# Preparing weight parts early and parking them in HBM: nine weight pairs of each FFN down projection in a float32 transformer trunk

## The chip, the cores and the metric

The kernel runs on one core of a Trainium2 chip. The metric is the device time of one execution in microseconds, taken as the median of repeated runs.

## The reference

Two post-norm layers over 256 positions of width 2048, all in float32. Each layer has a token mixer and a gated feed-forward network (FFN):

```python
for i in range(2):
    m = gmlp_mixer(x, ...) if i == 0 else mla_mixer(x, ...)
    x = layer_norm(ALPHA * x + m, ln_mix_g[i], ln_mix_b[i])
    f = conv_ffn(x, ...)
    x = layer_norm(ALPHA * x + f, ln_ffn_g[i], ln_ffn_b[i])

def conv_ffn(x, w_up, conv_w, conv_b, w_down):    # 2048 -> 2 x 5504 -> 2048
    h = causal_depthwise_conv3(x @ w_up, conv_w) + conv_b
    a, g = jnp.split(h, 2, axis=-1)
    return (jax.nn.silu(g) * a) @ w_down
```

The first mixer is a gMLP: `x @ w_in` (2048 to 12288), GELU, one half (v) normalized and mixed over 128-position windows, times the other half (u), then `w_out` (6144 to 2048). The second is multi-head latent attention.

## The kernel before

Float32 products are made from two parts. A value is split into a high part, rounded to the matmul's number format (a cast on ScalarE), and a low part, the rest (a subtraction on VectorE). A product is then three matmuls: high by high, low by high, high by low.

*Weights.* They are read once, in the order of use, as a list of chunks of 128 x 2048 (1 MB). The class `Feed` carries each through three steps: `_load` starts the transfer on SyncE's (SP's) queue into a tile `raw`; `_split` makes `wh` (L107, ScalarE) and `wl` (L108, VectorE); the caller uses the parts in matmuls (all recorded at L167). `feed.next(splits, loads)` keeps two to three chunks split and two more loaded ahead of the one in use. All these tiles, and the large activations too, come from one pool of 22 slots of 8 KB per partition (`big`), so a tile can start only when an older one in its slot is done with. The framework's scheduler settles the order of instructions on each engine and adds all semaphore waits.

*Down projections.* `down` makes a back projection (the gMLP's output, 48 blocks of k, or an FFN's second product, 43 blocks) in two halves of 1024 columns. A *unit* is a pair of k blocks in one half: a chunk of 2 x 1024 columns. Two blocks of k times two row blocks times two column blocks is a 2 x 2 matrix product, and there are two ways to make it. `Banks.eight` does the eight block products, 24 matmuls of 512 columns. `Banks.seven` uses seven products (a Strassen-Winograd form), 21 matmuls. It needs sums of weight blocks (`ts`, L122) and their parts `th`, `tl` besides `wh`, `wl` (L115, L116, in `Feed._seven`), and sums of activation blocks with their parts (`combine`). Eight PSUM banks take the products: four DIRECT ones (q3, p2, e, q4) and four OWN ones (p1, q5, p7, p6) that only the seven-product units use and that `rest` combines after the half's last one.

Which units use seven products is a table (`BACK`): 7 in each half of the gMLP's output, 6 in each half of an FFN's. The v part of the gMLP's first product uses them as well (`V_PAIRS`, `V_SEVEN`). The parts of the activations are made by the class `Sums`, four k blocks at a time (`quad`), and the sums for a pair once (`make`).

*Up projections.* 22 groups of output columns, four chunks each (the last two), with 256 positions as the moving operand: 16 matmuls of 512 and 16 of 256 columns per chunk. Convolution, SiLU and the product go into `act` tiles, six per FFN.

*Between them.* `boundary` finishes a normalization while the next product starts. `Norm` keeps the residual in two `big` slots; `restore` brings it back with the norm's scale and bias rows, during the next stage.

Of the kernel before, what the change touches and what calls it, by code (L numbers as in the profile page):

```python
# [15 lines left out]
P = 128  # L16
S = 256
# [42 lines left out]
def halves(n_k):  # L60

    one = [tuple(range(k, min(k + 2, n_k))) for k in range(0, n_k, 2)]
    two = []
    for q in BACK[n_k][1]:
        two += one[2 * q : 2 * q + 2][:: -1 if q in BACK[n_k][2] else 1]
    return [one, two]


class Feed:
# [3 lines left out]
    def __init__(self, nc, pool, chunks):  # L73
        self.nc, self.pool, self.chunks = nc, pool, chunks
        self.raw, self.parts = {}, {}
        self.loaded = self.split = self.used = 0

    def _load(self):
        ap, cols = self.chunks[self.loaded][:2]
        t = self.pool.tile([P, 2048], F32, tag="big", name=f"raw{self.loaded}")  # L80
# [12 lines left out]

    def _split(self):
        i = self.split
        cols, kind = self.chunks[i][1:]
# [5 lines left out]
        hi = self.pool.tile([P, 2048], F32R, tag="big", name=f"wh{i}")  # L102
        lo = self.pool.tile([P, 2048], F32R, tag="big", name=f"wl{i}")
# [14 lines left out]
    def _seven(self, i, raw):  # L118
# [4 lines left out]
        tile = lambda name, dt: self.pool.tile([P, 2048], dt, tag="big", name=f"{name}{i}")  # L123
# [8 lines left out]
        return wh, wl, th, tl  # L132

# [16 lines left out]
def trunk(ctx: ExitStack, tc: tile.TileContext, x, xT, gm_in, gm_wout, ffn_up, ffn_dn,  # L150
# [4 lines left out]
    big = ctx.enter_context(tc.tile_pool(name="big", bufs=22))  # L155
# [4 lines left out]
    def slot(shape, name, dt=F32):  # L160
        return big.tile(shape, dt, tag="big", name=name)
# [8 lines left out]
    chunks = []  # L170
# [6 lines left out]
    def back(w, n_k):  # L177

        for hf, units in enumerate(halves(n_k)):
            c = slice(hf * 1024, (hf + 1) * 1024)  # L180
            for u in units:
                if len(u) == 1:
                    chunks.append((w[u[0], :, c], 1024, "wide"))
                else:
                    chunks.append((w[u[0] : u[0] + 2, :, c].rearrange("k p c -> p k c"), 2048,
                                   "seven" if u[0] in BACK[n_k][0] else "wide"))

# [11 lines left out]
    feed = Feed(nc, big, chunks)  # L199

    idle = cpool.tile([P, 512], BF16, name="idle")
# [6 lines left out]

    def combine(name, o, k1, k2):


        t = tp.tile([P, 4, P], F32, tag="t2", name=f"xs{name}", bufs=6)
        b0, b1 = slice(0, P), slice(P, S)
        nc.vector.tensor_tensor(t[:, 0], k1[:, b1], k2[:, b1], ALU.subtract)
        nc.vector.tensor_tensor(t[:, 1], t[:, 0], k1[:, b0], ALU.subtract)
        nc.vector.tensor_tensor(t[:, 2], k1[:, b0], k1[:, b1], ALU.subtract)
        nc.vector.tensor_tensor(t[:, 3], k2[:, b0], t[:, 1], ALU.add)
# [3 lines left out]
        return [(o[:, 0, i], o[:, 1, i]) for i in range(4)]  # L221
# [40 lines left out]
    ones = cpool.tile([P, P], F32, name="ones")  # L262
    nc.gpsimd.memset(ones, 1.0)
# [45 lines left out]
    def sum_halves(acc, name):  # L309
        lo = tp.tile([P, S], F32, tag="t1", name=f"lo_{name}", bufs=8)  # L310
        nc.scalar.copy(lo, acc[:, S : 2 * S])  # L311
        h = tp.tile([P, S], F32, tag="t1", name=f"h_{name}", bufs=8)
# [3 lines left out]
    def split_act(src, name):  # L316

        t = tp.tile([P, 2 * S], F32R, tag="t2", name=name, bufs=6)
# [11 lines left out]
    class Banks:  # L330
# [17 lines left out]
        def seven(self, a, sums, wh, wl, th, tl):  # L348
            s1, s2, s3, s4 = sums
            self.to("p1", a[0][0], wh, wl, 0)  # L350
            self.to("q5", s1, th, tl, 0)
            self.to("p7", s3, th, tl, 512)
            self.to("p6", s2, th, tl, 1024)
            self.to("q3", s4, wh, wl, 512)
            self.to("p2", a[0][1], wh, wl, 1024)
            self.to("q4", a[1][1], th, tl, 1536)

        def rest(self):

            acc = self.acc  # L360
            p1, u2, u3, w, d = [tp.tile([P, 512], F32, tag="t2", name=f"{self.tag}{n}", bufs=6)
# [8 lines left out]
    class Sums:  # L370

        def __init__(self, src, tag):
            self.src, self.tag, self.rooms, self.got, self.quads = src, tag, [], {}, {}
            self.parts = {}

        def first(self):

            for k in range(4):  # L380
                x = self.src[0][:, k, :]
                t = tp.tile([P, 512], F32R, tag="t2", name=f"{self.tag}f{k}", bufs=6)
                nc.scalar.copy(t[:, 0:S], x)
                nc.vector.tensor_tensor(t[:, S : 2 * S], x, t[:, 0:S].bitcast(F32), ALU.subtract)
                self.parts[k] = t
            self.quads[0] = None

        def quad(self, q, n_k):
            if q in self.quads:
                return  # L390
            n = min(4, n_k - 4 * q)
            x = self.src[q // 2][:, 4 * (q % 2) : 4 * (q % 2) + n, :]
            t = slot([P, 4, 512], f"{self.tag}a{q}", F32R)
            nc.scalar.copy(t[:, 0:n, 0:S], x)
            nc.vector.tensor_tensor(t[:, 0:n, S : 2 * S], x, t[:, 0:n, 0:S].bitcast(F32), ALU.subtract)
            self.quads[q] = t
            for k in range(4 * q, 4 * q + n):
                self.parts[k] = t[:, k % 4, :]

        def make(self, k):  # L400
            if k in self.got:
                return
            n = len(self.got)
            if n % 2 == 0:
                self.rooms.append(slot([P, 2, 8 * P], f"{self.tag}xc{n}", F32R))
            x8 = self.src[k // 8]
            self.got[k] = combine(f"{self.tag}{n}", self.rooms[-1][:, n % 2, :], x8[:, k % 8, :], x8[:, k % 8 + 1, :])

    def down(n_k, src, tag, ln, sums, skew=SKEW):


        ln.begin()
        quads, sevens = sums.quads, BACK[n_k][0]
        late = []
        for hf, units in enumerate(halves(n_k)):
            n = len(units)
            last = [u for u in units if u[0] in sevens][-1]


            acc = Banks(f"{tag}{hf}", OWN + DIRECT if hf else DIRECT + OWN)  # L420
            for i, u in enumerate(units):
                left = n - 1 - i if hf == 1 else n
                for u2 in units[i : i + 3]:
                    sums.quad(u2[0] // 4, n_k)
                if i + 1 < n and units[i + 1][0] in sevens:
                    sums.make(units[i + 1][0])
# [3 lines left out]
                a = [[(sums.parts[k][:, b * P : (b + 1) * P], sums.parts[k][:, S + b * P : S + (b + 1) * P])  # L430
                      for k in u] for b in range(2)]
                if left < skew:
                    late.append((a, *got))
                elif u[0] in sevens:
                    acc.seven(a, sums.got[u[0]], *got)
# [3 lines left out]
                else:  # L439
                    acc.eight(a, *got)  # L440
                for q in [q for q in quads if q < u[0] // 4 and q not in [v[0] // 4 for v in units[i:]]]:
                    quads.pop(q)
            if hf == 0:
                for j, m in enumerate(DIRECT):
                    ln.piece(j // 2, j % 2, acc.acc[m])
                for q in [q for q in quads if q < units[-1][0] // 4]:
                    quads.pop(q)
# [68 lines left out]
    class Norm:  # L516


        def __init__(self, idx, res, last=False):
            self.idx, self.res, self.last, self.new = idx, res, last, None  # L520
            self.folded = set()

        def begin(self):
            if self.res is None:
                self.res = []
                for b in range(2):
                    t = slot([P, D], f"res{b}")
                    nc.sync.dma_start(t, x[b * P : (b + 1) * P, :])
                    self.res.append(t)
            self.stats = [st.tile([P, 4, 6], F32, tag="lnst", name=f"lnst{self.idx}_{b}") for b in range(2)]  # L530

# [11 lines left out]
        def restore(self, b, f):  # L543

            c = slice(f * 512, (f + 1) * 512)
            r = self.res[b][:, c]
            nc.vector.tensor_tensor(r, r, self.g[:, c], ALU.mult)
            nc.vector.tensor_tensor(r, r, self.b[:, c], ALU.add)

        def fold(self, b, f, part):  # L550

            r = self.res[b][:, f * 512 : (f + 1) * 512]
# [3 lines left out]
        def piece(self, b, f, acc):  # L556
            r = self.res[b][:, f * 512 : (f + 1) * 512]
# [12 lines left out]
        def scale(self, b, f):  # L570
            c = slice(f * 512, (f + 1) * 512)
            r = self.res[b][:, c]
# [587 lines left out]
```

## Time and profile before

| | |
|---|---|
| median of 3 runs | 2492.54 us (2492.25 to 2492.92) |
| the profiled execution | 2493.04 us, with a span of 2491.3 us |
| TensorE (PE) matmuls | 2475.7 us busy, 99% of the span |
| VectorE (DVE) | 1908.8 us, 77% |
| ScalarE (ACT) | 1388.8 us, 56% |
| GpSimd (POOL) | 2.9 us, no transfers issued |
| transfers | 480.27 MB, mean 193 GB/s |

The profile lists busy time for each engine, the chain of work that ended last, groups of instructions with their mean duration and the idle time before them, and transfers by issuing line with the time until the data has landed. The stretches by time from the span's start: v part of the gMLP to about 258 us, u part to 552, gMLP output to 800, first FFN up projection from 835 to 1285, its down projection to 1508, attention to 1770, second FFN up from 1804 to 2255, its down projection to the end.

### The profile page before, as it was taken

The numbers are of one execution on the slowest core, as the hardware profiler recorded it, in microseconds if no ns is written. First come the engines' busy times: TensorE is split into PE (matmuls) and PEld (weight loads), VectorE is DVE, ScalarE is ACT, GpSimd is POOL, SyncE is SP. The second block draws the span as 40 slices with busy tenths as digits, with TensorE's granted clock in tenths as the row PEclk, the third lists the DMA queues.
The fourth block names the chain that finished last, engine by engine and source line by source line (L and its number), as shares of the span: only waits on it lengthen the run. The fifth ranks groups of instructions, "written<-read, shape, count | busy, mean of one in ns | idle before, by whom it ended". The sixth has DMA issues, their size and how long they took to land.

```text
span 2491.3 us, 32651 instructions
## 1 busy us (share of the span) xinstructions
PE 2475.7 (99%) x13028; PEld 2128.3 (85%) x13028; DVE 1908.8 (77%) x2553; ACT 1388.8 (56%) x1891; POOL 2.9 (0%) x17
## 2 busy tenths in 40 slices
PE   9999999999999999999999999999999999999998
PEld 7888888888888888888888888988888888888886
DVE  7999866678888777666778997866487676669897
ACT  6566544445565755554655566565565555546553
POOL 0000000000000000000000000000000000000000
PEclk9999999999999999999999999999999999999999
DMA  7555554555566655555546674444465455555554
GB/s 295 198 187 214 196 186 157 181 196 194 186 217 222 223 186 200 188 184 185 187 155 201 219 247 169 168 153 168 156 231 191 169 202 182 180 179 179 209 192 181
DMA packets 86456, 480.27 MB, mean 193 GB/s; under 512 B 7712, under 2 KB 8480, under 8 KB 46752
## 3 DMA queue, kind: packets, MB, share of 16 engines
q1 hardware_dynamic: 86304, 478.19, 54.4%
q8 instruction: 102, 1.67, 0.3%
q14 instruction: 50, 0.41, 0.1%
HBM read 476.07 MB, written 2.10 MB: 192 GB/s over the span
## 4 chain that ended last, share of the span: by engine, by line
PE 96%; DVE 2%; issue 1%; DMA 1%; ACT 0%; SPq 0%; DVEq 0%; ACTq 0%
PE up L167 37%; PE u L167 11%; PE dn_q L167 9%; PE dn_p L167 6%; PE wo_q L167 4%; PE v_q L167 4%; PE mo L167 4%; PE dn_e L167 3%; PE v_p L167 3%; PE wo_p L167 3%; PE upf L167 2%; PE wo_e L167 2%; PE v_e L167 1%; PE mkv L167 1%; PE kn L167 1%; PE mq L167 1%
## 5 line engine op out<-in xcount | busy, mean ns | idle before, releaser
L108 DVE TENSOR_TENSOR wl<-raw,wh 128x1024 fp32r<-128x1024 f32 (+3 forms) x651 | 899.8, 1407 | 158.6 <-ACT wh L107 115.5
L107 ACT CAST wh<-raw 128x1024 fp32r<-128x1024 f32 (+3 forms) x651 | 761.8, 1201 | 284.9 <-DVE wl L108 120.4
L167 PE MATMUL up<-xhl,wh 128*128 128x512 f32 x2624 | 611.0, 390 | 0.0
L167 PEld LDWEIGHTS up<-xhl,wh 128*128 128x128 f32 x2624 | 487.4, 188 | 97.8
L167 PEld LDWEIGHTS up<-xhl,wl 128*128 128x128 f32 x2624 | 325.8, 192 | 6.4
L167 PE MATMUL up<-xhl,wl 128*128 128x256 f32 x2624 | 328.1, 283 | 0.0
L115 ACT CAST th<-ts 128x1536 fp32r<-128x1536 f32 x116 | 121.1, 1051 | 118.6 <-DVE ts L122 103.9
L167 PE MATMUL u<-xhl,wh 128*128 128x512 f32 x768 | 183.8, 393 | 0.3 <-DVE h_u L313 0.2
L167 PEld LDWEIGHTS u<-xhl,wh 128*128 128x128 f32 x768 | 141.3, 188 | 30.8 <-PE s L167 2.1
L116 DVE TENSOR_TENSOR tl<-ts,th 128x1536 fp32r<-128x1536 f32 x116 | 138.6, 1219 | 5.3 <-ACT th L115 4.5
L115 ACT CAST wh<-raw 128x1536 fp32r<-128x1536 f32 x58 | 85.9, 1480 | 43.2 <-DMA raw<-in_ffn_dn_dram 15.2
L116 DVE TENSOR_TENSOR wl<-raw,wh 128x1536 fp32r<-128x1536 f32 x58 | 101.6, 1752 | 5.4 <-ACT wh L115 5.4
L167 PEld LDWEIGHTS u<-xhl,wl 128*128 128x128 f32 x768 | 95.6, 192 | 2.0
L167 PE MATMUL u<-xhl,wl 128*128 128x256 f32 x768 | 96.7, 283 | 0.0
L167 PE MATMUL mo<-wh,oT 128*128 128x512 f32 x256 | 82.9, 404 | 0.0
L122 DVE TENSOR_TENSOR ts<-ts,raw 128x512 f32<-128x512 f32 x116 | 79.8, 688 | 1.8
L167 PE MATMUL wo_q<-wh,woa 128*128 128x512 f32 x256 | 78.8, 389 | 0.0
L122 DVE TENSOR_TENSOR ts<-raw 128x1024 f32<-128x1024 f32 x58 | 70.8, 1220 | 4.6 <-PE u L167 1.6
L313 DVE TENSOR_TENSOR h_0a<-up,lo_0a 128x256 f32<-128x256 f32 x41 | 17.3, 421 | 72.7 <-ACT lo_0a L311 72.7
L313 DVE TENSOR_TENSOR h_1a<-up,lo_1a 128x256 f32<-128x256 f32 x41 | 17.3, 421 | 71.9 <-ACT lo_1a L311 71.9
L167 PE MATMUL dn_q<-wh,dn0a 128*128 128x512 f32 x232 | 71.7, 390 | 0.0
L167 PE MATMUL dn_q<-wh,dn1a 128*128 128x512 f32 x232 | 71.5, 389 | 0.0
(497 smaller groups left out, 3924.6 us busy)
## 6 DMA issues: line engine op xcount, KB each, us to landing
raw<-in_ffn_up_dram SPq DMA_DIRECT2D x172, 1024.0 KB, 4.7
raw<-in_gm_in_dram SPq DMA_DIRECT2D x93, 1024.0 KB, 4.7
raw<-in_ffn_dn_dram SPq DMA_DIRECT2D x84, 1024.0 KB, 5.1
raw<-in_gm_wout_dram SPq DMA_DIRECT2D x48, 1024.0 KB, 5.2
raw<-in_ml_out_dram SPq DMA_DIRECT2D x16, 1024.0 KB, 4.8
raw<-in_ml_b_dram SPq DMA_DIRECT2D x14, 1024.0 KB, 4.8
raw<-in_ml_kv_dram SPq DMA_DIRECT2D x5, 864.0 KB, 4.4
lng<-in_ln_rows_dram SPq DMA_DIRECT2D x4, 1024.0 KB, 5.0
```

What stands on the lines that cost most here:

```text
L107: self.nc.scalar.copy(hi[:, c], raw[:, c])
L108: self.nc.vector.tensor_tensor(lo[:, c], raw[:, c], hi[:, c].bitcast(F32), ALU.subtract)
L115: self.nc.scalar.copy(hi, raw)
L116: self.nc.vector.tensor_tensor(lo, raw, hi.bitcast(F32), ALU.subtract)
L122: add = lambda o, a, b: self.nc.vector.tensor_tensor(o, a, b, ALU.add)
L167: nc.tensor.matmul(o, l, r, start=start, stop=stop, skip_group_check=True)
L313: nc.vector.tensor_tensor(h, acc[:, 0:S], lo, ALU.add)
```

## The change

*Parked parts.* Nine units in each FFN down projection, which were plain, now use seven products: pairs 4, 7, 10, 15, 19 in the first half and 19, 15, 10, 7 in the second. Their weights are not split when they are used. During the FFN's up projection, from its third group of columns on, the new `Feed.park` loads the unit's raw tile on POOL's queue, makes the four parts, and stores them in HBM, also on POOL's queue. One unit takes six chunks of the up projection (`jobs`, one step per chunk; a `yield` ends a step). In the down projection `_load` fetches the four parts on POOL's queue (`_fetch`) in place of the raw tile, and `_split` passes the unit by. The instructions of `park` are held at their place in the program's text (`keep_in_program_order`).

*Which units.* `BACK` becomes `PLAN`, a list of units with a kind each: e (eight products), s (seven), p (parked). The second half now runs through the pairs backwards. Pair 2 is no seven-product unit any more in the second half, in the gMLP's output and in both FFNs. In the built program TensorE has 12853 matmul instructions, before 12898; POOL issues 166 transfers, before none.

*Slots.* 22 `big` slots become 17 `big` and 6 `side`. Side slots hold the parts on their way in and out, and also the gMLP's six v tiles, five of its six pT tiles, the attention's qn and vv tiles, and the last two of six act tiles of each FFN. The small tile groups shrink: t1 from 8 to 6, t2 from 6 to 5, sbias from 2 to 1.

*Activation parts.* `Sums` becomes `Acts`: the parts are made per pair, three units ahead of use, and dropped unless a unit within the next 5, 9 or 6 (plain, seven, parked) needs them again. So the sums for a pair are made once for each half.

*Residual.* It is kept in halves of columns; after `restore` it is stored in HBM (`Norm.park`) and fetched on SP's queue eight units before a half ends. `restore` reads the scale and bias rows in pieces of 512 columns.

*Order.* In `seven` the products come in another order (those with `wh`, `wl` first); the v part's pairs run 0, 2, 1, 3, 5, 4, 6, 7 in place of 2, 0, 3, 1, 4, 5, 6, 7.

```diff
-V_PAIRS = [[0, 1, 2, 3, 4, 5, 6, 7]] + [[2, 0, 3, 1, 4, 5, 6, 7]] * 5
+V_PAIRS = [[0, 1, 2, 3, 4, 5, 6, 7]] + [[0, 2, 1, 3, 5, 4, 6, 7]] * 5
-BACK = {NF_GM: ((4, 10, 16, 22, 28, 34, 40), (11, 1, 2, 0, 4, 5, 7, 8, 10, 3, 6, 9), (5, 8)),
-        NF_FF: ((4, 10, 16, 22, 30, 34), (10, 1, 2, 0, 4, 5, 7, 8, 3, 6, 9), ())}
+T1, T2 = 6, 5
+SLOTS = {"big": 17, "side": 6}
+PLAN = {NF_GM: ("0e 1e 2s 3e 4e 5s 6e 7e 8s 9e 10e 11s 12e 13e 14s 15e 16e 17s 18e 19e 20s 21e 22e 23e",
+                "23e 22e 21e 20s 19e 18e 17s 16e 15e 14s 13e 12e 11s 10e 9e 8s 7e 6e 5s 4e 3e 2e 1e 0e"),
+        NF_FF: ("0e 1e 2s 3e 4p 5s 6e 7p 8s 9e 10p 11s 12e 13e 14s 15p 16e 17s 18e 19p 20e 21e",
+                "21e 20e 19p 18e 17s 16e 15p 14s 13e 12e 11s 10p 9e 8s 7p 6e 5s 4e 3e 2e 1e 0e")}
+KEEP = {"wide": 5, "seven": 9, "parked": 6}
...
+    def park(self, i):
...
+        tile = lambda n, dt: self.pool.tile([P, 2048], dt, tag="side", name=f"{n}{i}", bufs=SLOTS["side"])
...
+        def store(n, t, cols):
+            d = self.dram.tile([P, cols], F32, tag=f"kept{n}{i}", name=f"kept{n}{i}", bufs=1)
+            pin(nc.gpsimd.dma_start(d, t[:, 0:cols].bitcast(F32)))
+            kept[n] = d
...
+        raw = tile("praw", F32)
+        pin(nc.gpsimd.dma_start(raw.rearrange("p (k c) -> p k c", k=ap.shape[1]), ap))
+        yield
+        yield
+        yield
+        t = tile("pts", F32)
+        add(two(t, 0), two(raw, 512), raw[:, None, 0:512].to_broadcast([P, 2, 512]))
+        add(t[:, 1024:1536], t[:, 0:512], raw[:, 1024:1536])
+        add(t[:, 1536:2048], t[:, 1024:1536], raw[:, 1536:2048])
+        yield
+        for n, src, o, cols in (("w", raw, 512, 1536), ("t", t, 0, 2048)):
+            hi, lo = tile(f"p{n}h", F32R), tile(f"p{n}l", F32R)
+            pin(nc.scalar.copy(hi[:, 0:cols], src[:, o : o + cols]))
+            pin(nc.vector.tensor_tensor(lo[:, 0:cols], src[:, o : o + cols], hi[:, 0:cols].bitcast(F32), ALU.subtract))
+            store(f"{n}h", hi, cols)
+            store(f"{n}l", lo, cols)
+            if n == "w":
+                yield
+
+    def _fetch(self, i):
+        got = []
+        for n in ("wh", "wl", "th", "tl"):
+            d = self.kept[i].pop(n)
+            t = self.pool.tile([P, 2048], F32R, tag="side", name=f"f{n}{i}", bufs=SLOTS["side"])
+            self.nc.gpsimd.dma_start(t[:, 0 : d.shape[1]], d)
+            got.append(t)
+        return got
...
         def seven(self, a, sums, wh, wl, th, tl):
             s1, s2, s3, s4 = sums
+            self.to("q3", s4, wh, wl, 512)
+            self.to("p2", a[0][1], wh, wl, 1024)
             self.to("p1", a[0][0], wh, wl, 0)
+            self.to("q4", a[1][1], th, tl, 1536)
             self.to("q5", s1, th, tl, 0)
             self.to("p7", s3, th, tl, 512)
             self.to("p6", s2, th, tl, 1024)
-            self.to("q3", s4, wh, wl, 512)
-            self.to("p2", a[0][1], wh, wl, 1024)
-            self.to("q4", a[1][1], th, tl, 1536)
...
-                act[a // 8] = slot([P, 8, S], f"act{layer}_{a // 8}")
+                act[a // 8] = slot([P, 8, S], f"act{layer}_{a // 8}", tag="side" if a // 8 > 3 else "big")
...
+        jobs = park_all(feed.used + 2 * n_up)
         for gi in range(1, 22):
...
                 prod_a(acc, xhl, range(nk * c, nk * c + nk), hi, lo)
+                if gi > 1:
+                    next(jobs, None)
```

More of the change, by code (lines that the diff above doesn't have):

```diff
@@ L95, in _split @@
         i = self.split
-        cols, kind = self.chunks[i][1:]
+        cols, kind = self.chunks[i][1:3]
+        if kind == "parked":
+            self.split += 1
+            return
         raw = self.raw.pop(i)
@@ L177, in back @@
     def back(w, n_k):
-        for hf, units in enumerate(halves(n_k)):
+        for hf, units in enumerate(plan(n_k)):
             c = slice(hf * 1024, (hf + 1) * 1024)
[L181 to L186, printed above, removed]
+            for u, kind in units:
+                if 2 * u + 1 == n_k:
+                    chunks.append((w[2 * u, :, c], 1024, kind))
+                    continue
+                if kind == "parked":
+                    parked.append(len(chunks))
+                chunks.append((w[2 * u : 2 * u + 2, :, c].rearrange("k p c -> p k c"), 2048, kind))
     back(gm_wout, NF_GM)
@@ L422, in down @@
                 left = n - 1 - i if hf == 1 else n
[L423 to L426, printed above, removed]
+                for v2 in line[at : at + 3]:
+                    acts.make(*v2)
+                if i == n - 8:
+                    ln.fetch(hf)
                 got = feed.next(splits=2 if left > 5 or left == 0 else 3, loads=2 if left > 2 or left == 0 else 1)
@@ L429, in down @@
                     ln.prep()
-                a = [[(sums.parts[k][:, b * P : (b + 1) * P], sums.parts[k][:, S + b * P : S + (b + 1) * P])
-                      for k in u] for b in range(2)]
+                a, sums = acts.got[u]
                 if left < skew:
                     late.append((a, *got))
-                elif u[0] in sevens:
-                    acc.seven(a, sums.got[u[0]], *got)
+                elif kind == "wide":
+                    acc.eight(a, *got)
+                else:
+                    acc.seven(a, sums, *got)
                     if u == last:
@@ L438, in down @@
                             ln.fold(j // 2, 2 * hf + j % 2, t)
[L439 to L442, printed above, removed]
+                at += 1
+                for v2 in [v2 for v2 in acts.got if not any(v2 == w2 and n2 < KEEP[kind2]
+                                                            for n2, (w2, kind2) in enumerate(line[at:]))]:
+                    acts.got.pop(v2)
             if hf == 0:
@@ L703, in gate, with park_all @@
         nc.vector.tensor_tensor(pT[sl][:, pos, :], u, s, ALU.mult)
+    def park_all(until):
+        for i in [i for i in parked if feed.used < i < until]:
+            yield from feed.park(i)
+            yield
+    jobs = park_all(feed.used + 48 + 2 * len(PLAN[NF_GM][0].split()))
     for gi in range(12):
@@ L714, in trunk @@
         if gi == 10:
[L715 to L719 removed]
+            acts.make(*plan(NF_GM)[0][2])
+    ln = Norm(0, {})
+    acc, end = down(NF_GM, pT, "wo", ln, acts)
     def conv(layer, F, acc, name):
```

279 lines of the change are left out of this document (150 added, 129 removed).

## The prediction

> **What bounds the kernel now.** I read the page's busy times and its chain first, then who TensorE waits for, then the stretches of the span one by one, then the groups of instructions by shape, and the transfers last.
>
> ```profile
> span 2491.3 us, 32651 instructions
> ...
> PE 2475.7 (99%) x13028; PEld 2128.3 (85%) x13028; DVE 1908.8 (77%) x2553; ACT 1388.8 (56%) x1891; POOL 2.9 (0%) x17
> ...
> PE 96%; DVE 2%; issue 1%; DMA 1%; ACT 0%; SPq 0%; DVEq 0%; ACTq 0%
> ```
>
> TensorE (PE) is busy for 2475.7 of 2491.3 us and carries 96% of the chain. The list of its waits, and the stretches (v, gMLP output, first FFN up, first FFN down), say where it isn't:
>
> ```profile
> PE warm L167 <- POOL idle L202: 1.3, 1, 1.3
> PE wo_q L167 <- DVE wl L108: 1.1, 1, 1.1
> PE v_p L167 <- ACT wh L107: 1.0, 1, 1.0
> PE v_q L167 <- DVE v L637: 0.8, 2, 0.4
> ```
> ```profile
> core 0: us, PE busy (x) PEld busy (x) DVE busy (x) ACT busy (x) POOL busy (x), PEclk, DMA share, GB/s
> 4.00:258.00 254.00, 252.07 (x1100) 205.63 (x1099) 230.58 (x226) 163.18 (x200) 0.53 (x1) 1.00 0.62 228
> 552.00:800.00 248.00, 246.82 (x1089) 203.71 (x1089) 217.30 (x201) 139.15 (x112) 0.00 (x0) 1.00 0.60 204
> 835.00:1285.00 450.00, 450.00 (x2593) 398.54 (x2592) 314.80 (x482) 247.37 (x373) 0.00 (x0) 1.00 0.54 190
> 1285.00:1508.00 223.00, 223.00 (x988) 184.54 (x987) 199.09 (x187) 126.19 (x105) 0.32 (x2) 1.00 0.60 203
> ```
>
> All waits of one microsecond or more are one of each. In the FFN stretches PE has no gap at all, at a granted clock of 1.00. So time goes only if PE gets fewer instructions, and it is lost wherever the new work makes PE wait. VectorE (DVE) is the engine next to the limit: 91% of the v stretch, 88% of the gMLP output, 89% of the down projection, but 70% of the up projection. That difference is what the change uses.
>
> **The matmuls that go.** A unit is a pair of k blocks in one half of the columns. Done plainly it takes 24 matmuls of 512 columns, by the seven products 21. The chain near the end gives the price of one:
>
> ```profile
> 2457.67 4.08 PE dn_q L167 x18
> 2469.91 5.44 PE dn_e L167 x24
> ```
>
> 5.44/24 and 4.08/18 are both 0.2267 us. A plain unit is 5.44 us of PE, a seven-product unit 4.76 us. In each FFN nine plain units become parked seven-product units (9 x 3 = 27 matmuls fewer), and pair 2 of the second half turns plain (3 more): 24 fewer. The gMLP output loses its seven-product pair 2 in the second half: 3 more. Together 2 x 24 - 3 = 45 matmuls, and 45 x 0.2267 = 10.2 us, all of it on the path, since PE has no cover in these stretches.
>
> **The splitting that moves.** The rows by shape:
>
> ```profile
> L108 DVE TENSOR_TENSOR wl<-raw,wh 128x2048 fp32r<-128x2048 f32 x119 | 271.4, 2288 | 33.5 <-ACT wh L107 31.1 <-PE dn_q L167 1.0 <-ACT th L115 0.8
> L116 DVE TENSOR_TENSOR tl<-ts,th 128x1536 fp32r<-128x1536 f32 x58 | 101.7, 1753 | 5.3 <-ACT th L115 4.5
> L116 DVE TENSOR_TENSOR wl<-raw,wh 128x1536 fp32r<-128x1536 f32 x58 | 101.6, 1752 | 5.4 <-ACT wh L115 5.4
> L122 DVE TENSOR_TENSOR ts<-ts,raw 128x512 f32<-128x512 f32 x116 | 79.8, 688 | 1.8
> L122 DVE TENSOR_TENSOR ts<-raw 128x1024 f32<-128x1024 f32 x58 | 70.8, 1220 | 4.6 <-PE u L167 1.6 <-DMA raw<-in_gm_wout_dram 1.1 <-DMA raw<-in_ffn_dn_dram 1.0
> L116 DVE TENSOR_TENSOR tl<-ts,th 128x512 fp32r<-128x512 f32 x58 | 39.7, 685 | 0.0
> L395 DVE TENSOR_TENSOR dn1a<-act,dn1a 128x1024 fp32r<-128x1024 f32 x19 | 23.2, 1220 | 3.1 <-ACT dn1a L394 3.0
> L217 DVE TENSOR_TENSOR xsdn<-act,xsdn 128x128 f32<-128x128 f32 x12 | 3.4, 286 | 0.1
> L107 ACT CAST wh<-raw 128x2048 fp32r<-128x2048 f32 x119 | 226.8, 1912 | 62.8 <-DVE wl L108 12.3 <-PE wo_q L167 10.6 <-PE dn_q L167 10.6
> L115 ACT CAST wh<-raw 128x1536 fp32r<-128x1536 f32 x58 | 85.9, 1480 | 43.2 <-DMA raw<-in_ffn_dn_dram 15.2 <-PE dn_p L167 11.0 <-DVE wl L108 5.5
> ```
>
> In the up projection each parked unit adds three sums and two subtractions on DVE, 1.22 + 2 x 0.688 + 1.752 + 2.288 = 6.64 us, and two casts on ScalarE, 1.48 + 1.91 = 3.39 us. Nine units: 59.8 and 30.5 us. DVE goes from 314.8 to about 375 of 450 us (83%), ScalarE from 247 to 278 (62%). The cover is PE's 450 us; if DVE fell behind there, the next chunk's wl would be late, but 75 us stay free. The added wait is the first sum's, for its raw tile: the chunks' wl and h tiles are queued behind it on DVE. The load is issued three chunks ahead (some 16 us), against 5 us to land, so I price this at nothing, at most one late load. The traffic there grows by 9 x (1.05 + 3.67) MB, 94 GB/s on top of 190; raw tiles are asked for four chunks (4 x 5.6 us) ahead, so they hide it.
>
> In the down projection one seven-product and eight plain units leave DVE: 6.79 + 8 x 2.29 = 25.1 us. But the activations' parts are now made per pair, and the sums afresh for each half. Before, per FFN: some 20 subtractions for four blocks at 1.22, six sets of sums at 4 x 0.286 + 0.688 = 1.83, and four small subtractions at about 0.4, together near 37 us. After: 18 sets with direct parts at 4 x 0.286 + 2 x 0.688 = 2.52, and 22 plain ones at 0.688, together 60.5. Net 23.5 - 25.1 = -1.6 us: DVE keeps about 197.5 of what will be 217.6 us, 91%. The gMLP output rises by some 7 us to 90%. The v stretch ran at 91% with 1.9 us lost, so I take no general stall here.
>
> **Slots.** 22 common slots become 17 and 6 side ones. The v tiles, five of six pT tiles, qn and vv go to the side, and so do the last two act tiles of each FFN. In the v stretch the feed has 11 slots from the start instead of 16 falling to 10, and two seven-product pairs now stand in a row: 2 x 6.79 of DVE against 2 x 4.76 of PE, a debt of 4.1 us. Bounds: the waits of 1.0 and 0.8 us in the v stretch go (-1.8), or each of five groups loses 1 us (+5); I take +1. The gMLP output gets more room, as pT no longer takes the feed's: its wait of 1.1 us goes, -1 (0 to -1.1). SP's queue loses 18 raw loads and gains small ones for ln rows and the residual, with 40 us to spare.
>
> **The fetches, the one uncertain term.** A parked unit's four parts are 2 x 0.786 + 2 x 1.049 = 3.67 MB. In the first half two side slots hold act tiles, so four are left, one unit's parts: the next unit's fetch waits on POOL's queue until PE has done with the slots. In the order 4p 5s 6e 7p, wh and wl are free after nine of 21 matmuls (2.04 us). From there to the next unit's first matmul are 2.72 + 4.76 + 5.44 = 12.9 us, and to its th 2 us more: 15. In these 15 us two raw tiles of 1.05 MB come too: 5.77 MB. What the transfers can do, and what one takes by itself:
>
> ```profile
> 12.00:15.00 3.00, 2.94 (x13) 1.95 (x12) 2.38 (x4) 2.68 (x4) 0.00 (x0) 1.00 1.04 420
> 24.00:27.00 3.00, 3.00 (x15) 2.48 (x14) 2.73 (x4) 2.30 (x2) 0.00 (x0) 1.00 1.03 412
> 33.00:36.00 3.00, 3.00 (x15) 2.48 (x14) 3.00 (x3) 3.00 (x4) 0.00 (x0) 1.00 1.00 418
> ```
> ```profile
> raw<-in_ffn_dn_dram SPq DMA_DIRECT2D x84, 1024.0 KB, 5.1
> ```
>
> With a deep queue they carry 412 to 420 GB/s: 5.77 MB in 13.7 us. A tile lands in 5.1 us, of which 2.5 are its bytes, so 2.6 are lag: 16.3 us against 15, 1.3 late, less what the raw tiles have moved before. I take 0.75 us for each short gap; there are four (4p-7p-10p, in two FFNs): +3. Lower end 0. The upper end is the down stretch's row: 203 GB/s at a share of 0.60 would be 338 at a full one, 17.1 + 2.6 = 19.7, 4.7 late, 19 us over four. The longer gaps (four or five units, 20.5 and 25 us, 7.9 MB with a residual half) need 18.8 + 2.6 at 420: about even.
>
> The Trainium skill, SBUF — State Buffer, section "Summary: rules for kernel authors", says to reckon with about 358 GB/s between HBM and SBUF. By it, as an estimate, a short gap takes 16.1 + 2.6 us and the four cost 15, for about 2497 us. The trace differs with its 412 to 420, and the measurement decides.
>
> **The sum.** The profiled execution took 2493.04 us for its span of 2491.3, 0.5 over the median of 2492.54. 2493.04 - 10.2 + 1 - 1 + 3 = 2485.8; less 0.5 for the median: about 2485 us. A difference of 0.2%, 5 us, is about what a measurement of this kernel can tell from no change; faster means below 2487.5.
>
> **The rivals.** *Fetches too slow (slower).* Place: TensorE's first matmul or first th matmul of the parked pairs 7 and 10. It decides where the queues together move less than about 380 GB/s: then each short gap is over 2.5 us late (5.77/0.38 + 2.6 = 17.8 against 15) and the four eat the 10.2 us. At 338 GB/s the four cost 19, and the four-unit gap 5 in each FFN: 2492.5 - 10.2 + 29 = 2511. For it: no row of before shows a transfer from POOL's queue, or one that writes fp32r from f32. Against: the 420. Chance 0.23.
>
> *POOL's issues held up by DVE.* These rows show DVE work of two kinds:
>
> ```profile
> L574 DVE TENSOR_SCALAR res<-res,lnmv,lnrs 128x512 f32<-128x512 f32 x24 | 12.4, 541 | 0.2
> L676 DVE TENSOR_SCALAR v<-v,vmv,vrs 128x1024 f32<-128x1024 f32 x12 | 8.8, 807 | 0.0
> ```
>
> 512 elements more cost 266 ns here, against 532 in the two-input rows (688 to 1220). If every DVE instruction held an issue, four in a row would wait up to 4 x 2.29 = 9.2 us, then 5 for the last part's bytes beside a raw tile and 2.6 of lag: 16.8 against 15.4, with the waits before it some 2.5 late per short gap: 10 us, about 2492. The Trainium skill, same page and section, speaks against moving transfers to this queue: it advises the hardware queues because POOL cannot write descriptors while DVE runs its two-port modes. It names copies and tensor_scalar for these, not tensor_tensor. The down stretch has next to no instruction of the fast kind (the 24 stand at the norms), so I give it 0.12.
>
> *The v stretch starves on 11 slots.* Five groups lose 1 us each, and the fetches 3: about 2489. Chance 0.11.
>
> *The change doesn't shorten PE,* because something else paced the down projections: PE is busy for 223.00 of 223 there, so hardly; it is part of the second rival's chance.
>
> **How the numbers follow.** Forecast 0.54, nearly all below 2487.5. Faster: 0.50 of it and 0.04 of the third rival. Same: 0.04, 0.09 of the second, 0.07 of the third. Slower: the first rival and 0.03 of the second. The range begins at 2480.5, with no late fetch and the v stretch's waits gone (2492.5 - 10.2 - 1.8), and ends at 2512, the slow rival's price, since the two signs both hold much of the chance; what lies above is under 0.1. The likeliest case's own range is 2481 to 2488.
>
> **What would show it.** Right: some 45 matmuls fewer, the down stretches some 5 us shorter each, the up stretches at 450 us with DVE near 83%, PE's waits under 1 us apiece. Wrong: rows in which PE waits for a DMA of fwh, fth or ftl by more than 2.5 us at pairs 7 or 10; the up stretch longer than 451; waits on v or h_u beyond 2 us.

## The result and the profile after

The changed kernel takes 2510.28 us in the median of four runs (2505.52 to 2513.39), the kernel before 2492.39 beside it: a ratio of 1.0070 (95% interval 1.0052 to 1.0087). It is 17.9 us slower; 2485 had been forecast. The profiled execution took 2510.28 us for a span of 2508.4.

From the page of the changed kernel: the span, the busy times, the transfer queues.

```profile
span 2508.4 us, 33417 instructions
...
PE 2474.3 (99%) x12983; PEld 2122.7 (85%) x12983; DVE 2002.8 (80%) x2805; ACT 1430.9 (57%) x1982; POOL 94.8 (4%) x183
...
q1 hardware_dynamic: 85440, 463.51, 51.5%
q0 software_dynamic: 26208, 155.20, 15.9%
```

TensorE has its 45 matmuls fewer, yet is busy for as long as before (2475.7). POOL's queue, q0, carries 155 MB that were not there. The stretches of the first FFN's up and down projections (start and end in us, then length, and for each engine busy time and instructions, last the granted clock, the transfer engines' share and GB/s):

```profile
835.00:1285.00 450.00, 449.60 (x2589) 397.79 (x2587) 363.25 (x519) 272.98 (x388) 28.25 (x50) 1.00 0.80 297
1285.00:1505.00 220.00, 211.03 (x908) 172.03 (x909) 184.16 (x239) 114.01 (x119) 17.21 (x34) 0.98 0.82 297
```

Nothing is lost up to 1285 us: the first matmul of the down projection starts at 1285.0, before at 1284.9. From there to the attention's first matmul are 236.3 us, before 226.7. The second down projection with the end takes 244.1 us, before 236.5. The clock is 0.98 there, and PE, which had no gap before, stands still for 9 of 220 us. Who it waits for (us, times, longest):

```profile
PE dn_q L223 <- ACT wh L119: 7.3, 4, 4.4
PE dn_q L223 <- DMA ftl<-kepttl: 6.3, 4, 3.2
PE dn_q L223 <- DVE wl L120: 3.1, 4, 1.6
```

The row of ftl is the wait that the prediction had priced at 3: two of these waits lie at pair 7 and 10 of the first FFN (1324 and 1341 us), the others at the same places of the second. Of the rows of wh and wl, 9.2 us belong to one plain unit, pair 12 in the second half of each FFN: 5.5 us from 1443 and 3.7 us from 2424. The other 1.2 us stand at the first unit of each down projection, in e2 and e11 below as well, so they are no part of this loss. The chain that ended last shows what stands behind the late plain units (start, us, what):

```profile
2377.95 9.14 DMA raw<-in_ffn_dn_dram
2387.16 1.92 ACT wh L119
...
2401.40 6.29 DMA raw<-in_ffn_dn_dram
...
2412.08 12.14 DMA raw<-in_ffn_dn_dram
2424.30 1.91 ACT wh L119
2426.23 2.30 DVE wl L120
2428.58 2.08 PE dn_q L223 x4
```

A raw tile that lands in 5.1 us in the kernel before is 12.1 us on its way, and cast, subtraction and TensorE follow on its heels. It is no fault of ScalarE or VectorE that the list of waits names them. The median over all of the down projections' raw tiles is 7.9:

```profile
raw<-in_ffn_dn_dram SPq DMA_DIRECT2D x66, 1024.0 KB, 7.9
...
ftl<-kepttl POOLq DMA_DIRECT2D x18, 1024.0 KB, 9.9
```

The same thing at 1440 us, in stretches of 5 us. Two raw tiles asked for at 1432.8 and 1435.1 land at 1445.5 and 1447.8; beside them run four parts that POOL asked for from 1429.4 to 1432.7.

```profile
1435.00:1440.00 5.00, 4.93 (x21) 3.95 (x22) 3.52 (x4) 1.35 (x3) 0.00 (x0) 1.00 1.05 402
1440.00:1445.00 5.00, 3.17 (x14) 2.28 (x13) 0.00 (x0) 0.00 (x0) 0.00 (x0) 1.00 1.03 365
1445.00:1450.00 5.00, 1.35 (x3) 0.63 (x3) 2.48 (x3) 2.42 (x2) 0.00 (x0) 0.54 1.02 389
1450.00:1455.00 5.00, 5.00 (x12) 3.94 (x13) 5.00 (x8) 3.46 (x3) 0.00 (x0) 0.50 0.27 109
```

Read it by rows: the transfer engines are full (1.05, 1.03, 1.02) while VectorE and ScalarE run dry, then PE; and when the data is there, PE runs at half its clock (12 matmuls in 5 us instead of 22). The clock was halved for 10.24 us from 1445.4, and for 3.41 us each from 2322.7 and 2428.5: 17.07 us. In some 3.7 of them PE stood still anyway, so about 6.7 us are lost to the clock (the 8.5 in the expectations below is half of 17.07, without that).

### The profile page after: what moved, and what is told of

It reads as the page before. It is cut to its first block, busy times and chain, and to the rows that moved or that the text cites. A ratio compares the mean times of both kernels' runs of the same rounds, so it can differ in the third digit from the quotient of the medians.

```text
span 2508.4 us, 33417 instructions
## 1 busy us (share of the span) xinstructions
PE 2474.3 (99%) x12983; PEld 2122.7 (85%) x12983; DVE 2002.8 (80%) x2805; ACT 1430.9 (57%) x1982; POOL 94.8 (4%) x183
## 5 line engine op out<-in xcount | busy, mean ns | idle before, releaser
L120 DVE TENSOR_TENSOR wl<-raw,wh 128x1024 fp32r<-128x1024 f32 (+3 forms) x636 | 868.2, 1385 | 251.1 <-ACT wh L119 213.9
L119 ACT CAST wh<-raw 128x1024 fp32r<-128x1024 f32 (+3 forms) x636 | 734.4, 1184 | 412.0 <-DMA raw<-in_ffn_up_dram 95.7
L127 ACT CAST th<-ts 128x1536 fp32r<-128x1536 f32 x110 | 115.5, 1052 | 84.9 <-DVE ts L134 75.8
L128 DVE TENSOR_TENSOR tl<-ts,th 128x1536 fp32r<-128x1536 f32 x110 | 131.0, 1217 | 1.9 <-ACT th L127 1.7
L128 DVE TENSOR_TENSOR wl<-raw,wh 128x1536 fp32r<-128x1536 f32 x55 | 96.3, 1751 | 0.5 <-PE wo_p L223 0.4
L223 PE MATMUL v_q<-wh,xhl 128*128 128x512 f32 x224 | 69.4, 391 | 2.2 <-ACT wh L119 2.2
L223 PE MATMUL v_p<-wh,xhl 128*128 128x512 f32 x192 | 59.9, 390 | 0.3 <-ACT wh L119 0.3
L223 PEld LDWEIGHTS v_q<-wh,xhl 128*128 128x128 f32 x224 | 41.8, 188 | 12.0 <-ACT wh L119 3.6
L223 PEld LDWEIGHTS mo<-wh,oT 128*128 128x128 f32 x256 | 45.3, 189 | 7.2
L223 PE MATMUL mo<-wl,oT 128*128 128x512 f32 x128 | 50.3, 393 | 0.0
## 6 DMA issues: line engine op xcount, KB each, us to landing
praw<-in_ffn_dn_dram POOLq DMA_DIRECT2D x18, 1024.0 KB, 14.8
kepttl<-ptl POOLq DMA_DIRECT2D x18, 1024.0 KB, 10.8
```

Source lines behind the costliest of these rows:

```text
L119: self.nc.scalar.copy(hi[:, c], raw[:, c])
L120: self.nc.vector.tensor_tensor(lo[:, c], raw[:, c], hi[:, c].bitcast(F32), ALU.subtract)
L127: self.nc.scalar.copy(hi, raw)
L128: self.nc.vector.tensor_tensor(lo, raw, hi.bitcast(F32), ALU.subtract)
L223: nc.tensor.matmul(o, l, r, start=start, stop=stop, skip_group_check=True)
```

## The experiments

All kernels are the changed one with the edit shown; only e12 is the kernel before. Theory A was from the start that POOL's fetches take the transfer engines from SP's raw loads; theory B that 17 slots are too few, so that raw tiles are asked for too late whatever POOL does.

| run | edit | us | ratio to the kernel before (95% interval) |
|---|---|---|---|
| e1 | no pair parked | 2497.52 | 1.0016 (1.0007 to 1.0026) |
| e2 | high parts fetched only | 2485.05 | 0.9967 (0.9955 to 0.9978) |
| e3 | six pairs, six units apart | 2507.70 | 1.0058 (1.0043 to 1.0073) |
| e4 | fetches on SP's queue | 2501.49 | 1.0034 (1.0021 to 1.0047) |
| e5 | POOL rows 2 KB | 2510.18 | 1.0069 (1.0054 to 1.0084) |
| e6 | raw rows 8 KB | 2496.34 | 1.0015 (1.0006 to 1.0024) |
| e7 | both | 2499.54 | 1.0026 (1.0016 to 1.0035) |
| e8 | both, no short gap | 2485.54 | 0.9970 (0.9958 to 0.9981) |
| e9 | no short gap | 2513.21 | 1.0083 (1.0068 to 1.0099) |
| e10 | raw rows 8 KB, no short gap | 2486.84 | 0.9971 (0.9960 to 0.9983) |
| e11 | as e10, nine parked | 2484.91 | 0.9966 (0.9954 to 0.9979) |
| e12 | kernel before, raw rows 8 KB | 2493.26 | 0.9999 (0.9991 to 1.0008) |
| e13 | POOL rows 2 KB, no short gap | 2490.30 | 0.9990 (0.9980 to 1.0000) |
| e14 | POOL rows 1 KB, no short gap | 2491.11 | 0.9995 (0.9985 to 1.0004) |

### Is it the fetches? (e1, e2)

```diff
# e1: in PLAN every p of the FFNs becomes e
-"0e 1e 2s 3e 4p 5s 6e 7p 8s 9e 10p ... 15p ... 19p 20e 21e"
+"0e 1e 2s 3e 4e 5s 6e 7e 8s 9e 10e ... 15e ... 19e 20e 21e"
# e2: in _fetch
+            if n in ("wl", "tl"):
+                got.append(got[-1])
+                continue
```

> All nine parked pairs of each FFN are done plainly (24 matmuls instead of 21) and nothing is parked or fetched; the rest of the change (side slots, 17 common slots, parts per pair, order of products) stays. 54 matmuls more than the changed kernel, 9 more than the kernel before: 9 x 0.2267 = +2.0 us, and -0.8 for the two small waits that went. Theory A (POOL's fetches take the transfer engines from SP's raw loads): the late raw tiles and the halved clock are gone with the fetches, 2493.5 us (2492 to 2496), down stretches without a PE wait over 1.5 us. Theory B (with 17 common slots the raw tiles are asked for too late, whatever POOL does): the waits on wh and wl in the second halves stay, 5 us and a stretch of halved clock per FFN, so 2502 or more.

> Of a parked pair only the high parts wh and th are fetched back; TensorE reads them again in the place of wl and tl, so the number of matmuls is that of the changed kernel, while the fetched bytes and the side slots of a pair are halved (1.84 MB instead of 3.67). The low parts are left out of the result. Theory A: ftl waits (6.3 us in the profile), late raw tiles (10.4) and halved clock (8.5 us lost) go nearly whole, 2510 - 25 = 2485 us (2483 to 2489). Theory B: the raw tiles stay late, 10.4 and most of 8.5 us remain, about 2503.

Measured: 2497.5 and 2485.05 us. e2 leaves the low parts of the parked weights out of its result. In e1 the down projections have no wait over 1.1 us and full clock throughout:

```profile
PE dn_q L223 <- DVE dn01wx L459: 1.1, 1, 1.1
...
PE dn_q L223 <- ACT wh L119: 0.8, 2, 0.4
```

With the slots, the order and the activation parts of the change, and without its transfers, nothing is late: theory B is refuted. The time is 3.9 us over the kernel before, though, not 1.1, and outside of what was expected: 2.0 are the nine matmuls more and 1.1 the wait shown. Another 2.0 are waits that the kernel before does not have and that e2 and e11 have as well, 1.2 at the first unit of each down projection and 0.8 in the gMLP's u part; the gMLP output's wait of 1.1 went. e2 has all of the change's matmuls and half of its fetched bytes, and takes what the prediction gave for the whole change. It halves the side slots in use as well, so by itself it doesn't say whether bytes or slots matter.

### More room between the parked pairs, and one queue (e3, e4)

```diff
# e3
+"0e 1e 2s 3e 4p 5s 6e 7e 8s 9e 10p 11s 12e 13e 14s 15e 16p 17s 18e 19e 20e 21e"
+"21e 20e 19p 18e 17s 16e 15e 14s 13p 12e 11s 10e 9e 8s 7p 6e 5s 4e 3e 2e 1e 0e"
# e4
-            self.nc.gpsimd.dma_start(t[:, 0 : d.shape[1]], d)
+            self.nc.sync.dma_start(t[:, 0 : d.shape[1]].bitcast(F32), d)
```

> Six parked pairs per FFN instead of nine, with six units between two of them in place of three to five; pair 7 of the first half and two others are plain. 18 matmuls more than the changed kernel, 4.1 us. Theory A: no short gap is left, the waits on ftl go, and of the late raw tiles at most one per FFN remains: 2485 + 4.1 = 2489 us, up to 2494. Theory B: the waits on wh and wl stay as they are, 2503.

> The parts are fetched through SP's queue, in one line with the raw tiles and in the order of their use, instead of through POOL's; everything else is as in the changed kernel. Theory A: nothing overtakes a raw tile any more, so the late raw tiles of the second halves and the halved clock go; in the first halves SP itself now waits for side slots, so the short gaps stay and may cost a little more: 2487 to 2497 us. Theory B: a queue that also waits for side slots asks for raw tiles later still: 2512 or more.

Measured: 2507.7 and 2501.5 us, both outside of what either theory gave. e3 was my clearest miss. Its waits:

```profile
PE dn_q L223 <- DVE tl L128: 4.3, 4, 1.7
PE dn_q L223 <- DVE wl L120: 3.6, 4, 1.6
...
PE dn_q L223 <- ACT th L127: 1.7, 1, 1.7
```

No ftl is late any more, but the raw tiles are as late as ever. With room between the pairs all four side slots are free at once, so POOL asks for four parts within 4 us (1309.6 to 1312.9), and two raw tiles asked for beside them, at 1310.2 and 1314.2, take 10.7 and 15.0 us. This burst is no denser than the changed kernel's first (1309.0 to 1312.2), but beside that one there is one late raw tile and not two: the pairs that are no longer parked need raw tiles themselves. And where the short gaps make the changed kernel's parts come two by two (1324.0 and 1328.8), wide spacing lets all four come at once.

e4 puts all into one line. Its waits on wl are many and small, but the scheduler, which had other transfers to plan with, also ordered TensorE's work at the boundary in another way: the norm's transposes (lnt) start 1.9 us behind the down projection's last matmul, in the changed kernel 4.5 us ahead of it. Three rows of its waits:

```profile
PE dn_q L223 <- DVE wl L120: 4.1, 9, 1.1
...
PE mq L223 <- ACT xhl L667: 2.0, 1, 2.0
PE lnt L660 <- DVE res L647: 2.0, 1, 2.0
```

The two waits of 2.0 at the boundary, with 6.83 us of halved clock behind them, go with that order. So e4 shows that overtaking matters (2510 to 2501), not how much.

### Rows (e5, e6, e7)

Why 10.7 us, twice the 5.1 of a raw tile alone? A raw tile's rows in memory are 4 KB (1024 columns of a block), a part's 6 or 8 KB. If an engine takes a row from one queue and then one from the other, the raw tile gets a third: 1.05 MB at 140 GB/s and 2.6 of lag make 10.1 us. That is theory C; A' says that the queues share by bytes.

```diff
# e5: rows of 2 KB for the parts
-            d = self.dram.tile([P, cols], F32, ...)
+            d = self.dram.tile([cols // 512, P, 512], F32, ...)   # stored and fetched as "k p c -> p k c"
# e6: rows of 8 KB for the raw tiles (layout of the input)
-    ffn_dn = a["ffn_w_down"].reshape(2, NF_FF, P, D)
+    dn = np.concatenate([a["ffn_w_down"], np.zeros((2, P, D), np.float32)], axis=1)
+    ffn_dn = dn.reshape(2, (NF_FF + 1) // 2, 2, P, 2, 1024).transpose(0, 4, 1, 3, 2, 5).reshape(2, 2, -1, P, 2048)
# a chunk is then read as w[half, pair], in park too
# e7: both
```

> The kept parts lie in memory so that each row of a transfer is 2 KB instead of 6 or 8 KB; the same bytes go through POOL's queue at the same places. Theory C (the engines take a row from one queue, then a row from the other, so a raw tile with its 4 KB rows gets a third of the rate against POOL's 8 KB rows): a raw tile now gets two thirds beside POOL, lands in about 1.05/0.27 + 2.6 = 6.4 us instead of 10 to 12, most of the late raw tiles (10.4 us) and of the halved clock (8.5 us lost) go, the waits on ftl (6.3) stay or grow by a little for POOL's own issues: 2493 us (2490 to 2498). Theory A' (the two queues share by bytes, whatever the rows): raw tiles as late as before, 2510 us or a few more.

> The weights of the down projection lie in memory so that a raw tile's rows are 8 KB instead of 4 KB; POOL's rows stay at 6 and 8 KB. Theory C: a raw tile gets about half the rate beside POOL instead of a third, 1.05/0.2 + 2.6 = 7.8 us: about half of the late raw tiles' 10.4 us and of the clock's 8.5 go, 2500 us (2495 to 2505). Theory A': 2510 us, as the changed kernel.

> Both: raw tiles with 8 KB rows, POOL's parts with 2 KB rows. Theory C: a raw tile gets four fifths beside POOL, about 5.8 us to land; the late raw tiles and the halved clock behind them go, the short gaps' ftl waits stay (6.3 us or a little more, as the parts now give way): 2491 us (2488 to 2496). Theory A': 2510 us.

Measured: 2510.2, 2496.3 and 2499.5 us. By the times alone e5 went as A' gave, e6 as theory C, and e7 fell between the two. The rates show that the rows do shift the shares. From the transfer records of the first down projection (1300 to 1500 us), over the microseconds in which each queue moved over 20 KB and both over 330:

| run | raw rows, part rows | SP GB/s | POOL GB/s |
|---|---|---|---|
| changed kernel | 4 KB, 6 and 8 KB | 161 | 244 |
| e5 | 4 KB, 2 KB | 233 | 162 |
| e6 | 8 KB, 6 and 8 KB | 204 | 210 |
| e7 | 8 KB, 2 KB | 271 | 132 |

The Trainium skill, DMA: Bandwidth & Descriptors, section "Queues, rings and completion order", says that an engine goes round the queues that have work and takes a whole packet from one before the next. The table agrees as far as the shares are not by bytes alone; that a turn would be 9 to 17 descriptors is not shown by any run here. By turns of one row each, as theory C has it, SP would get 33 to 40, 67, 50 to 57 and 80% of the sum; it gets 40, 59, 49 and 67%. So the shares move with the rows, but not the whole way, and the changed kernel's rows gave SP 49% in e9 (192 of 390 GB/s). What else sets them stays open.

Yet e5 gained nothing. Its waits:

```profile
PE dn_q L225 <- DMA ftl<-kepttl: 10.9, 4, 4.7
PE dn_q L225 <- DVE wl L120: 3.6, 4, 1.6
...
PE dn_q L225 <- ACT wh L119: 2.0, 3, 1.2
```

Against the changed kernel the raw tiles' waits fell from 9.2 to 4.4 us (without the 1.2 at the first units) and ftl's rose from 6.3 to 10.9. In the short gaps parts and raw tiles are both due at once, and whoever gives way is late. e6, with a smaller shift, gains 14 us; its ftl waits are 4.0, those of e7 6.4. Its raw tiles also move faster by themselves: where SP's queue is alone it moves 391 GB/s with 4 KB rows (kernel before) and 415 with 8 KB (e12).

### The short gap (e8, e9, e10, e11) and a control (e12)

```diff
# e8, e9, e10: pair 7 of the first half is plain
-"0e 1e 2s 3e 4p 5s 6e 7p 8s 9e 10p ..."
+"0e 1e 2s 3e 4p 5s 6e 7e 8s 9e 10p ..."
# e8 with the rows of e7, e9 with none, e10 with the rows of e6
# e11: as e10, and in the second half
-"... 7p 6e 5s 4e 3e 2e 1e 0e"
+"... 7p 6e 5s 4p 3e 2e 1e 0e"
# e12: the kernel before with the layout of e6, its chunks read as w[half, pair]
```

> As the one with both rows, and pair 7 of each first half is plain, so that no two parked pairs stand three units apart: 6 matmuls more (1.4 us) and the ftl waits go. Theory C: 2485 + 1.4 + 1 = about 2488 us (2486 to 2491), faster than the kernel before. Theory A': the ftl waits go, the late raw tiles and the clock stay, about 2505 us.

> The changed kernel with pair 7 of each first half plain, rows as they were (raw tiles 4 KB, parts 6 and 8 KB): 6 matmuls more, 1.4 us, no parked pairs three units apart in the first halves. Theory C (late raw tiles come from sharing by rows): the ftl waits (6.3 us) and one window of halved clock (1.7) go, the late raw tiles of the second halves and their clock stay: 2510 - 6.6 = about 2503.5 us (2500 to 2506). Theory D (it is the short gaps that make the transfers fall behind, and the raw tiles are late only in their wake): nearly all goes, about 2487 us.

> Raw tiles of the down projection with 8 KB rows, pair 7 of each first half plain, POOL's parts with their 6 and 8 KB rows as in the changed kernel. Theory C, if half the rate is enough for a raw tile: 2486 us (2485 to 2489), no wait of TensorE over 1.5 us in the down stretches. If POOL's 2 KB rows are needed too: raw tiles late by some us, 2490 us or more.

> As the one with raw rows and no gap, and pair 4 of each second half is parked too, so that there are nine parked pairs per FFN again: 6 matmuls fewer, 1.4 us less, 2484.5 us, if nothing waits. If the last sums of a half, now one unit later, hold up the norm behind it, or pair 4's parts come late three units after pair 7's: 2486 us or more.

> The kernel before, with the weights of the down projection laid out for 8 KB rows and nothing else. TensorE has no wait there, so no change: 2492.5 us (within 0.05%). If 8 KB rows are worth something by themselves in this program: 2490 us or less.

Measured: 2485.5, 2513.2, 2486.8, 2484.9 and 2493.3 us. e9 and e10 have the same units and the same bytes; only the raw tiles' rows differ, and the times differ by 26.4 us. (The rows of the raw tiles that POOL loads in the up projection change with them; PE is busy for 449.60 and 449.87 of 450 us there.) The longest rows of e9's waits, where e10 has none over 1.1 us in the down projections:

```profile
PE dn_q L223 <- DVE wl L120: 6.0, 6, 1.6
PE dn_q L223 <- ACT wh L119: 4.4, 5, 1.4
PE dn_q L223 <- DVE tl L128: 3.4, 2, 1.7
```

The same stretch of both, first e9, then e10:

```profile
1310.00:1315.00 5.00, 5.00 (x24) 4.14 (x23) 4.90 (x6) 3.64 (x6) 1.06 (x2) 1.00 0.96 336
1315.00:1320.00 5.00, 5.00 (x24) 4.14 (x23) 2.69 (x3) 1.21 (x3) 0.00 (x0) 1.00 1.05 365
...
1325.00:1330.00 5.00, 3.94 (x18) 2.93 (x16) 2.18 (x3) 1.85 (x2) 0.00 (x0) 1.00 0.81 249
1330.00:1335.00 5.00, 2.71 (x8) 1.92 (x9) 4.86 (x9) 2.08 (x5) 0.00 (x0) 0.88 0.57 226
```
```profile
1310.00:1315.00 5.00, 5.00 (x24) 4.14 (x23) 5.00 (x6) 3.67 (x5) 1.41 (x3) 1.00 0.90 329
1315.00:1320.00 5.00, 5.00 (x24) 4.14 (x23) 4.82 (x7) 2.96 (x4) 0.00 (x0) 1.00 1.06 421
...
1325.00:1330.00 5.00, 5.00 (x24) 4.14 (x23) 4.66 (x8) 2.17 (x4) 0.00 (x0) 1.00 0.76 272
1330.00:1335.00 5.00, 5.00 (x24) 4.14 (x23) 4.93 (x11) 2.98 (x4) 0.00 (x0) 1.00 0.64 226
```

In e9 VectorE falls to 2.69 of 5 us at 1315 (it waits for raw tiles), and PE loses its place ten microseconds later; in e10 neither stops. Two raw tiles that e9 asks for at 1309.1 and 1313.1 take 10.8 and 14.9 us; those of e10, at 1309.8 and 1313.8, 7.9 and 10.0. The nearer of my two expectations for e9 missed by 10 us, the other by 26: without pair 7's fetch its ftl wait goes, but a raw tile of its own comes in its place, and later parts come four at once, as in e3. e8 adds to e10 the parts' shorter rows and is about as fast, so these are not needed. e11, as fast as e2 within the noise, has the change's 12983 matmuls, all of its bytes, and no wait over 0.4 us in the down projections, where the changed kernel has its three rows of 7.3, 6.3 and 3.1:

```profile
PE dn_q L223 <- ACT wh L119: 0.8, 2, 0.4
PE mq L223 <- ACT xhl L671: 0.4, 1, 0.4
PE dn_q L223 <- DVE wl L120: 0.4, 2, 0.2
```

e12, the kernel before with the same rows, shows no change, though a raw tile lands there in 4.7 us instead of 5.1: where TensorE waits for no raw tile, the rows are worth nothing.

### Share or rate? (e13, e14)

```diff
# e13: e9 with the parts' rows of e5; e14: the same with rows of 1 KB (256 columns)
```

> Pair 7 of each first half plain, raw tiles with their 4 KB rows, POOL's parts with 2 KB rows. Against the run without the short gap this changes only who gets the engines while both queues are full: SP's share rose from 161 to 233 GB/s when POOL's rows went to 2 KB, while the rate of both together went from 405 to 395. Theory E (a raw tile's share of the engines decides): the late raw tiles go as they did with 8 KB raw rows, 2486 to 2490 us. Theory F (the lower rate of 4 KB rows, 391 against 415 GB/s alone, decides, whoever goes first): the loss stays, 2508 us or more.

> The same with POOL's rows of 1 KB. Theory E: a raw tile's share rises further, 2486 to 2490 us, unless the parts themselves, slower with such rows, come late at the parked pairs (waits on ftl of some us each). Theory F: 2510 us or more.

Measured: 2490.3 and 2491.1 us, against e9's 2513.2. With the raw tiles' rows at 4 KB and only the parts' rows smaller, SP's part beside POOL goes from 192 of 390 GB/s to 235 of 394 and 251 of 384, the two raw tiles land in 7.9 and 9.9 us in both, and 23 and 22 of e9's 26 us go. Both times are just above what theory E gave (2486 to 2490); in e14 one part is late, an ftl by 1.5 us. So it is the share of the engines (theory E), and not the lower rate of 4 KB rows, which both kept. The 3.5 us that e13 keeps over e10 fit the lower rate (both queues together 394 GB/s, in e10 414), but this was not tried by itself.

## Why the prediction was wrong

*Right.* The 45 matmuls and their price: in the runs with the change's 12983 matmuls and no late transfer, e2 and e11, PE is busy for 2464.9 and 2465.2 us, 10.8 and 10.5 less than before (10.2 had been reckoned). That they take 2485.05 and 2484.91 us, just the forecast of 2485, is luck in part: the forecast had 3 us for late fetches in it, which these runs don't pay, and lacked the 2.0 us of waits at the first units and in the u part. The up projection pays nothing: VectorE 363.25 of 450 us (375 had been reckoned), ScalarE 272.98 (278), TensorE 449.60. But this was close: the parked raw tiles landed in 14.8 us in the median, not 5, against a lead reckoned at some 16. The gMLP output's wait of 1.1 went; the v stretch, where 1 us had been feared, ends as it did (258.3 us, before 258.2), so the rival that had it starve falls too. POOL's issues weren't held up by VectorE, and that rival falls. The 18 issues of one kind, in nanoseconds (least, median, most):

```profile
L185 POOL DMA_DIRECT2D fwh<-keptwh x18: 528/531/551, 1154.1 to 2414.0; - x18
```

*The step that failed* is the fetches, called the one uncertain term, at +3 us. It had three faults.
1. Its own price, 0.75 us for each short gap: the four cost 6.3.
2. It reckoned the two queues as one line with enough bandwidth (5.77 MB in 13.7 us), in which only the parts could be late. For the raw tiles the text had only that SP's queue has 40 us to spare. But where both queues were full, the raw tiles, with the shorter rows, got 161 of 405 GB/s, and plain units waited 9.2 us for them. That term stood at nothing.
3. No price at all for a stop beyond its own length: halved clock after it, about 6.7 us.

6.3, 9.2 and 6.7 make 22.2; the changed kernel's span is 25.1 longer than e2's with the same matmuls. Of the other 2.9, 0.6 are two more rows of waits (tl and fth). About 1.6, by estimate, lie at the edges of the stops: the last matmul before each is recorded with 0.39 us where the steps between matmuls are 0.2267, so each of some ten stops cost 0.16 us more than its row says. The rest stays open. (The expectation of e2 also came to 25, from 6.3, 10.4 and 8.5: two of the three were too high.) Against before it is e2's -8.0 and these 25.1: +17.1 us from 2491.3 to 2508.4.

*The slow rival* came out at nearly the measured time, 2511, for another reason. Its condition, under 380 GB/s for both queues, did not hold, if not by much: they moved 405 together in the microseconds picked for the table, those above 330, near the 412 to 420 reckoned with, and 385 in the mean of the three full stretches shown from 1435 us. The Trainium skill, SBUF — State Buffer, section "Summary: rules for kernel authors", gives 358 GB/s; the trace is above it in both. Of the loss at its place, pairs 7 and 10, there were 6.3 us. The forecast's test, a wait of over 2.5 us for a part at these pairs, was met once (3.2). It looked in the wrong place for most.

## What to carry to other kernels

A prefetch on a second queue takes bandwidth from the loads that are due now, even where the sum of bytes fits. Count, for each queue, how long a transfer takes while the other is full; shares here moved with the length of the rows, so give the urgent stream the longer rows (e10) or the prefetch the shorter ones (e13), and keep the prefetch's own deadline apart from it (e5 against e13). More room between prefetches did not help by itself (e3, e9): the fetches came in bursts all the same, and what was no longer prefetched had to be loaded beside them.

In the changed kernel TensorE's stops of three to six microseconds cost about half as much again in clock (5.5 us cost 3.5 more, 3.2 cost 1.6, 3.7 cost 1.7), so that belongs in the price.

## What the runs showed of the hardware

The halved clock follows a fixed grid. In these traces its starts and ends within a run lie whole multiples of 3.413 us apart. Sorting each run's PE gaps into such windows: in all 13 windows in which PE stood still for 61% or more, the next window ran at half clock; of the 19 with 40 to 56%, two were followed by it (56% in e9, 47% in e3), the others were not, one with 51% in e3 among them. So these runs give no sharp limit. The Trainium skill, TensorE: Matmul & The Clock Gate, Part 1, gives this window (free-running, some 3.4 us) and names an idle window as what halves the clock. The traces agree on the window and show that a window need not be idle throughout: a gap of 1.6 us was enough where it fell within one (from 2408.0 in e3), and two of 1.7 us in e3, spread over two windows at 1330 to 1334, had no effect, while two of 1.7 us in e9 (1329 to 1333), a little more of them in one window, had.

The mean share of the transfer engines does not tell a stalled stretch from a good one. In e11's first down projection it is 0.80, in the changed kernel 0.82:

```profile
1285.00:1505.00 220.00, 219.59 (x968) 181.00 (x968) 195.05 (x255) 117.97 (x122) 17.16 (x34) 1.00 0.80 306
```
